# Stores of a routing table, issued by ScalarE in place of SP

## The chip, the cores and the metric

The program runs on one core of a Trainium2 chip. A core has TensorE (PE, matrix products), VectorE (DVE), ScalarE (ACT), GpSimd (POOL) and SyncE (SP). Each takes its instructions in order from a queue of its own, and they meet in semaphores. PE, DVE and ACT compute; SP only issues DMAs here, and ACT and POOL issue some too. The metric is device microseconds for one execution of the whole program, the median of several runs.

## The reference

The reference is a network on 512 tokens of width 1024, in float32: two blocks of modulated FFN, token mixing (gated MLP, differential attention, sparse attention) and FFN, then a second block whose feed-forward part is PEER, a choice among 16384 experts. The change lies in PEER, of which this is the core:

```python
q = (xf @ wq).reshape(t, PEER_HEADS, 2, PEER_DKEY // 2)
scores = jnp.einsum("thpc,hpnc->thpn", q, sub_keys)
s_top, i_top = lax.top_k(scores, PEER_TOPK)            # 16 of 128, two sides
cand_s = s_top[:, :, 0, :, None] + s_top[:, :, 1, None, :]
best_s, best_pos = lax.top_k(cand_s, PEER_TOPK)        # 16 experts a head
gates = jax.nn.softmax(best_s, axis=-1)
u = jnp.take(u_tab, expert_idx); vv = jnp.take(v_tab, expert_idx)
act = gelu(einsum("cd,chkd->chk", xc, u)) * gates
out = einsum("chk,chkd->cd", act, vv)
```

So each token has 8 heads with 16 experts each, 128 pairs of an expert number and a gate.

## The kernel before

A float32 product is done as three products of two halves: each weight tile of 512 KB is loaded by SP into `raw` (4 buffers), ACT copies its high half to `wh` (L265), DVE the rest to `wl` (L266), both with three buffers, and PE runs 24 matmuls for one projection (`proj`, L288): 8 with `yh` and `wh`, 8 with `yl` and `wh`, 8 with `yh` and `wl`.

The first 128 tokens fetch the rows of their experts (GpSimd's indirect loads `row`, DVE's products `vacc`). For the other 384 the kernel computes all 16384 experts, in 128 units of 128, and weights them with a gate that is zero for experts not chosen. In `peer()` the loop of L1855 to L1863 does this for the first 94 units while the gates are not yet known: a projection with the weights `pu`, the gelu `hg` on ACT, and a store `acts` of `hg` to DRAM, issued by ACT (L1859). Beside it, in portions, runs the generator `route()` that makes the gates.

`route()` lays the gates out as a table of 128 x 128 experts by token. It takes the 384 tokens in 6 blocks of 64. For 4 tokens of a block (a group, 16 in a block) DVE compares numbers and makes two selection matrices `o1` and `o2` (L1686, L1688; both stand as `o` in the rows), ACT scales the second by the gates, `og` (L1690, four instructions), PE multiplies both to `gp` in PSUM (L1697, four matmuls), and ACT copies `gp` into the block's tile `st` (L1698). `st` is 128 x 128 x 64 float32 with one buffer. At a block's end four stores of 1 MB each, `gates`, bring `st` to DRAM (L1711); that of the last block stays where it is. The next block's first copy into `st` has to wait until these stores have landed. Three groups are in flight at a time, as far as the buffers go. Later the gates are read back, by unit (`gs` L1847, `gq` L1892).

What runs when is set in two steps: by credits in Python, `routed()` and `gather()`, which say how many portions of `route()` and of the row fetch go with each projection, and by the scheduler of the language, which sets each engine's order from its own costs of the instructions. It places a store's issue as an instruction of the engine that issues it. There is no order written by hand.

Of the kernel before, what the change touches and what calls it, by code (L numbers as in the profile page):

```python
# [198 lines left out]
class Net:  # L199
# [1404 lines left out]
    def route(self, X, G, begun):  # L1604


        nc = self.nc
        best, pos, itop, numbers, iis = {}, {}, {}, {}, {0: self.ii0}
        for quad in range(4):
# [3 lines left out]
            for i in range(4):  # L1613
                q = self.x[4 + i]
# [4 lines left out]
            for t in range(NT):  # L1619
# [27 lines left out]
                if t == 0:  # L1647
                    yield from self.resolve(best[0], pos[0], itop[0], self.ii0, quad * 2, 2)
                    q = slice(quad * 32, quad * 32 + 32)
# [9 lines left out]
        for n, (t, a, b) in enumerate(BLOCKS):  # L1659
            for v in (t, BLOCKS[n + 1][0] if n + 1 < len(BLOCKS) else t):  # L1660
                if v not in iis:
                    iis[v] = self.blk(name="ii")
                    yield from self.resolve(best[v], pos[v], itop[v], iis[v], 0, 8)
            if t not in numbers:
                ii = iis[t]
                tp = self.bank("tp", "T")
                nc.tensor.transpose(tp[:, :P], ii[:, :P], self.ident)
                nc.tensor.transpose(tp[:, P:2 * P], ii[:, P:2 * P], self.ident)
                nc.tensor.transpose(tp[:, 2 * P:3 * P], best[t], self.ident)
                tr = self.blk(name="tr")  # L1670
                nc.vector.tensor_copy(tr[:, :384], tp[:, :384])
                trb = tr[:, 384:].bitcast(BF)[:, :P]
                nc.vector.tensor_copy(trb, tr[:, P:2 * P])
                numbers[t] = tr, trb
                yield "turn", 2
            tr, trb = numbers[t]
            st = self.stage.tile([P, NE, BT], F32, name="st", tag="st", bufs=1)
            left = []

            def four(v):  # L1680
                return v.rearrange("p (a b) -> p a b", b=P)

            for q in range(a, b, 4):
                o1, o2 = self.blk(name="o1"), self.tmp.tile([P, P, 4], BF, name="o2", tag="t", bufs=6)
                og = self.blk(name="og")
                nc.vector.tensor_tensor(four(o1), self.iota[:, None, :].to_broadcast([P, 4, P]),  # L1686
                                        tr[:, q:q + 4, None].to_broadcast([P, 4, P]), op=OP.is_equal)
                nc.vector.tensor_tensor(o2, self.iota4, trb[:, None, q:q + 4].to_broadcast([P, P, 4]), op=OP.is_equal)  # L1688
                for i in range(4):
                    nc.scalar.activation(og[:, i * P:(i + 1) * P], o2[:, :, i], AF.Copy,  # L1690
                                         scale=tr[:, 2 * P + q + i:2 * P + q + i + 1])

                def outer(o1=o1, og=og, q=q):
                    ps = self.bank("gp", "T")
                    for i in range(4):
                        c = slice(i * P, (i + 1) * P)
                        nc.tensor.matmul(ps[:, c], lhsT=o1[:, c], rhs=og[:, c], start=True, stop=True)  # L1697
                    nc.scalar.activation(st[:, :, q - a:q - a + 4], ps.rearrange("p (t e) -> p e t", t=4), AF.Copy)  # L1698

                left.append(outer)  # L1700
                if len(left) > 3:
                    left.pop(0)()
                yield "hot", 2
            for f in left:
                f()
                yield "late", 2
            if n == len(BLOCKS) - 1:
                self.last_gates = st
            else:
                for q in range(4):  # L1710
                    nc.sync.dma_start(G[:, n, q * 32:(q + 1) * 32], st[:, q * 32:(q + 1) * 32])  # L1711
                yield "late", 2

    def chosen(self, XN, acc):
# [288 lines left out]
```

## Time and profile before

| | us |
|---|---|
| median of 3 runs | 3659.66 (3652.52 to 3664.91) |
| the profiled execution | 3655.58 |
| its span, first to last instruction | 3653.8 |

The mean clock that TensorE was granted is 0.991 of full speed. The profile names engines and lines: "L1711" is line 1711 of the kernel, "st<-gp" an instruction that fills `st` from `gp`; a row of the timeline may stand for several like instructions ("x8"), and in brackets is the idle time ahead of it with what ended it. A matmul of the program in float32 can stand as two rows' instructions: a `gp` group of four is x8. "SPq" and "ACTq" are the issues of DMAs by SP and ACT. The stores in question are issued between 2686 and 2914 us; the loop with `route()` beside it runs until about 2940 us, and the last phase, with the gates read back, from there to the end.

### The profile page before, as it was taken

To read this page: it belongs to the slowest core of one execution; us is meant where nothing else is said; L and a number is where in the kernel's file an instruction comes from. 1 tells how busy PE (TensorE), PEld (TensorE's weight loads), DVE (VectorE), ACT (ScalarE), POOL (GpSimd) and SP (SyncE) were. 2 spreads that over 40 slices of the span, in tenths; PEclk is the share of its full clock that TensorE was granted. 3 is DMA by queue.
4 is the path that set the end of the run, shared out by engine and by line. 5 is a ranking of instruction groups with operands and counts; after the bars stand their busy time and mean duration, and the time that the engine had idled before them with its cause. 6 is when DMAs were issued, how large, how long until landed. Compare 5 with 4: busy or idle time off the path is not lost. (4 is left out here: it accounts for less than half of the span.)

```text
span 3653.8 us, 49253 instructions
## 1 busy us (share of the span) xinstructions
PE 3545.1 (97%) x18265; PEld 3011.7 (82%) x18265; DVE 2394.0 (66%) x4791; ACT 1564.9 (43%) x2770; POOL 371.1 (10%) x358
## 2 busy tenths in 40 slices
PE   7999999999999999999999999899999999999998
PEld 6888876788888888766888887788999999988886
DVE  6555587665563334776533377598998777788786
ACT  4332466433233323465433254333477753344333
POOL 0000100000000001000000000011331234432220
PEclk9999999999999999999999999999999999999999
DMA  7566330266653333400233321245887888899994
GB/s 250 185 187 200 113 100 18 64 197 195 199 187 104 98 91 111 128 30 24 93 93 95 100 84 64 75 147 187 270 292 287 302 280 315 311 338 355 328 325 143
DMA packets 260896, 636.49 MB, mean 174 GB/s; under 512 B 83696, under 2 KB 118816, under 8 KB 258096
## 3 DMA queue, kind: packets, MB, share of 16 engines
q1 hardware_dynamic: 207312, 474.35, 40.1%
q0 software_dynamic: 39808, 140.52, 11.2%
q10 hardware_dynamic: 13536, 18.49, 1.4%
q8 instruction: 143, 2.34, 0.3%
q14 instruction: 97, 0.79, 0.1%
HBM read 591.71 MB, written 41.55 MB: 173 GB/s over the span
## 5 line engine op out<-in xcount | busy, mean ns | idle before, releaser
L265 ACT ACTIVATE wh<-raw 128x1024 fp32r<-128x1024 f32 (+2 forms) x620 | 645.8, 1043 | 1135.2 <-PE proj L288 864.5
L266 DVE TENSOR_TENSOR wl<-raw,wh 128x1024 fp32r<-128x1024 f32 (+2 forms) x620 | 743.9, 1202 | 497.5 <-ACT wh L265 358.9
L288 PE MATMUL proj<-yh,wh 128*128 128x512 f32 (+1 forms) x2744 | 644.8, 374 | 6.0 <-ACT hg L1853 2.0
L288 PE MATMUL proj<-yh,wl 128*128 128x512 f32 (+1 forms) x2744 | 627.2, 370 | 11.7 <-DVE wl L266 11.6
L288 PE MATMUL proj<-yl,wh 128*128 128x512 f32 (+1 forms) x2744 | 628.9, 370 | 0.0
L288 PEld LDWEIGHTS proj<-yh,wl 128*128 128x128 f32 x2744 | 502.8, 188 | 83.0 <-DVE wl L266 15.4
L288 PEld LDWEIGHTS proj<-yh,wh 128*128 128x128 f32 x2744 | 499.5, 188 | 81.3 <-ACT hg L1853 3.3
L288 PEld LDWEIGHTS proj<-yl,wh 128*128 128x128 f32 x2744 | 503.8, 188 | 67.6
L540 DVE SCALAR_TENSOR_TENSOR scr<-raw,cact 128x1024 bf16<-128x1024 f32 x128 | 156.6, 1224 | 133.1 <-DMA raw<-in_wada 132.6
L1836 PE MATMUL acc<-wl,yh 128*128 128x512 f32 x756 | 234.2, 391 | 2.4 <-DVE wl L266 2.4
L1836 PE MATMUL acc<-wh,yh 128*128 128x512 f32 x756 | 233.8, 390 | 1.3 <-ACT wh L265 1.2
L1836 PE MATMUL acc<-wh,yl 128*128 128x512 f32 x756 | 233.3, 390 | 1.6 <-DVE yl L272 1.6
L1744 POOL DMA_INDIRECT row<-in_purows,c x128 | 156.5, 1223 | 521.5 <-DVE row L1728 276.8
L672 DVE TENSOR_TENSOR ga<-sg,proj 128x512 f32<-128x512 f32 x88 | 60.5, 687 | 227.0 <-PE proj L288 223.2
L1744 POOL DMA_INDIRECT row<-in_pv,c x128 | 167.0, 1305 | 371.0 <-DVE vacc L1736 245.3
L277 PE MATMUL proj<-yl,wh 128*128 128x256 f32 (+1 forms) x552 | 177.0, 330 | 10.8 <-DVE yl L399 7.1
L278 PE MATMUL proj<-yh,wl 128*128 128x256 f32 (+1 forms) x552 | 173.8, 323 | 2.2 <-DVE wl L266 2.2
L276 PE MATMUL proj<-yh,wh 128*128 128x256 f32 (+1 forms) x552 | 164.6, 328 | 7.8 <-ACT yh L645 6.3
L1836 PEld LDWEIGHTS acc<-wl,yh 128*128 128x128 f32 x756 | 141.2, 188 | 34.7 <-DVE wl L266 5.4
L1836 PEld LDWEIGHTS acc<-wh,yl 128*128 128x128 f32 x756 | 141.8, 188 | 32.1 <-DVE yl L272 2.1
L1836 PEld LDWEIGHTS acc<-wh,yh 128*128 128x128 f32 x756 | 141.2, 188 | 29.9 <-ACT wh L265 2.1
L1736 DVE SCALAR_TENSOR_TENSOR vacc<-row,act,vacc 128x1024 f32<-128x1024 f32 x127 | 162.6, 1280 | 0.7
(465 smaller groups left out, 5178.0 us busy)
## 6 DMA issues: line engine op xcount, KB each, us to landing
raw<-in_wada SPq DMA_DIRECT2D x144, 512.0 KB
raw<-in_pu SPq DMA_DIRECT2D x128, 512.0 KB
raw<-in_pv SPq DMA_DIRECT2D x128, 512.0 KB
raw<-in_wg SPq DMA_DIRECT2D x84, 512.0 KB
raw<-in_wu SPq DMA_DIRECT2D x84, 512.0 KB
raw<-in_wd SPq DMA_DIRECT2D x64, 512.0 KB
gates<-st SPq DMA_DIRECT2D x20, 1024.0 KB
acts<-hg ACTq DMA_DIRECT2D x94, 192.0 KB
```

Of the source, the lines that this page charges most:

```text
L265: nc.scalar.activation(h[:, :n], raw[:, :n], AF.Copy)
L266: self.latest = nc.vector.tensor_sub(l[:, :n], raw[:, :n], h[:, :n].bitcast(F32)).ins
L276: mm(out, lhsT=lh, rhs=rh, start=start, stop=False)
L277: mm(out, lhsT=lh, rhs=rl, start=False, stop=False)
L278: mm(out, lhsT=ll, rhs=rh, start=False, stop=stop)
L288: self.nc.tensor.matmul(ps, lhsT=w[:, k * P:(k + 1) * P], rhs=X[c + k][part], start=c + k + i == 0, stop=i == 2 and c + k == nk - 1)
L540: nc.vector.scalar_tensor_tensor(scr, raw, 1.0, self.cact, op0=OP.mult, op1=OP.mult, accum_out=self.mod[:, l, j:j + 1])
L672: nc.vector.tensor_mul(a, sg, p[1])
L1736: nc.vector.scalar_tensor_tensor(acc, row, a, acc, op0=OP.mult, op1=OP.add)
L1744: nc.gpsimd.indirect_dma_start(out=row, out_offset=None, in_=tables[kind], in_offset=bass.IndirectOffsetOnAxis(ap=self.experts[:GT, s:s + ...
L1836: nc.tensor.matmul(acc[q], lhsT=a[:, t * P:(t + 1) * P], rhs=half(w, m), start=q not in started, stop=end and i == 2)
```

## The change

The four stores of a block are issued by ACT instead of SP, 20 stores in all:

```diff
--- before.py
+++ after.py
@@ -1708,7 +1708,7 @@
                 self.last_gates = st
             else:
                 for q in range(4):
-                    nc.sync.dma_start(G[:, n, q * 32:(q + 1) * 32], st[:, q * 32:(q + 1) * 32])
+                    nc.scalar.dma_start(G[:, n, q * 32:(q + 1) * 32], st[:, q * 32:(q + 1) * 32])
                 yield "late", 2
 
     def chosen(self, XN, acc):
```

Besides the issue itself the scheduler now orders ACT, PE and DVE otherwise around each of the five stores. On SP the 20 issues are gone and nothing else moves, but that the first read of `gs` stands three loads earlier.

ACT around block 2's store, before. The names are: `og_23368` and on the groups of block 3, `st_23365` the tile of block 3, `hg_23387`, `hg_23448` and `hg_23515` the gelus of three projections, `wh_23586` and on the high halves of the weights of the next ones.

```order
L1690 ACTIVATE og_23377<-o2_23376,tr_23362 128x128 x4
L1853 ACTIVATE hg_23387<-proj_23388 128x384
L265 ACTIVATE wh_23586<-raw_23584 128x1024
L1859 DMA acts_19126<-hg_23387 128x384
L1690 ACTIVATE og_23423<-o2_23422,tr_23362 128x128 x4
L265 ACTIVATE wh_23638<-raw_23636 128x1024
L1853 ACTIVATE hg_23448<-proj_23449 128x384
L1859 DMA acts_19126<-hg_23448 128x384
L1690 ACTIVATE og_23432<-o2_23431,tr_23362 128x128 x4
L1690 ACTIVATE og_23484<-o2_23483,tr_23362 128x128 x4
L265 ACTIVATE wh_23705<-raw_23703 128x1024
L1698 ACTIVATE st_23365<-gp_23439 128x128x4
```

The splits `wh` of three units stand ahead of the first copy into the new tile `st_23365`.

The same place after the change, from the store on:

```order
L1711 DMA gates_19125<-st_22814 128x2048 x4
L1690 ACTIVATE og_23368<-o2_23367,tr_23362 128x128 x4
L1690 ACTIVATE og_23377<-o2_23376,tr_23362 128x128 x4
L1853 ACTIVATE hg_23387<-proj_23388 128x384
L1698 ACTIVATE st_23365<-gp_23439 128x128x4
L1859 DMA acts_19126<-hg_23387 128x384
L1690 ACTIVATE og_23423<-o2_23422,tr_23362 128x128 x4
L1690 ACTIVATE og_23432<-o2_23431,tr_23362 128x128 x4
L1853 ACTIVATE hg_23448<-proj_23449 128x384
L1698 ACTIVATE st_23365<-gp_23491 128x128x4
```

and, behind one more `acts` store:

```order
L1690 ACTIVATE og_23484<-o2_23483,tr_23362 128x128 x4
L1690 ACTIVATE og_23499<-o2_23498,tr_23362 128x128 x4
L1698 ACTIVATE st_23365<-gp_23506 128x128x4
L1853 ACTIVATE hg_23515<-proj_23516 128x384
L1698 ACTIVATE st_23365<-gp_23558 128x128x4
L1859 DMA acts_19126<-hg_23515 128x384
L1690 ACTIVATE og_23551<-o2_23550,tr_23362 128x128 x4
L1690 ACTIVATE og_23566<-o2_23565,tr_23362 128x128 x4
L1698 ACTIVATE st_23365<-gp_23573 128x128x4
L265 ACTIVATE wh_23586<-raw_23584 128x1024
```

The first copy into `st_23365` now stands one `hg` behind the store, and the split `wh_23586` stands behind five of these copies.

PE at the same place before, from the end of the projection that ran when block 2 was done; `o_23366` and on are groups of block 3:

```order
L288 MATMUL proj<-yh,wl 128x384 x8
L1697 MATMUL gp<-og,o_23366 128x128 x4
L288 MATMUL proj<-yh,wh 128x384 x8
L288 MATMUL proj<-yl,wh 128x384 x8
L288 MATMUL proj<-yh,wl 128x384 x8
L1697 MATMUL gp<-og,o_23375 128x128 x4
L1697 MATMUL gp<-og,o_23421 128x128 x4
L288 MATMUL proj<-yh,wh 128x384 x8
L288 MATMUL proj<-yl,wh 128x384 x8
L288 MATMUL proj<-yh,wl 128x384 x8
L1697 MATMUL gp<-og,o_23430 128x128 x4
L1697 MATMUL gp<-og,o_23482 128x128 x4
```

PE after, from the end of the second projection behind that place:

```order
L288 MATMUL proj<-yh,wh 128x384 x8
L288 MATMUL proj<-yl,wh 128x384 x8
L288 MATMUL proj<-yh,wl 128x384 x8
L1697 MATMUL gp<-og,o_23366 128x128 x4
L1697 MATMUL gp<-og,o_23375 128x128 x4
L1697 MATMUL gp<-og,o_23421 128x128 x4
L1697 MATMUL gp<-og,o_23430 128x128 x4
L1697 MATMUL gp<-og,o_23482 128x128 x4
L1697 MATMUL gp<-og,o_23497 128x128 x4
L1697 MATMUL gp<-og,o_23549 128x128 x4
L1697 MATMUL gp<-og,o_23564 128x128 x4
L288 MATMUL proj<-yh,wh 128x384 x8
```

The groups stood one or two between two projections of 24 matmuls; now three projections (two of them and the rest of one) stand in a row, eight groups follow together, and the next projection after them. Behind blocks 4 and 5 the order of ACT and PE is changed in the same way.

## Rows read from the trace of the kernel before

**Rows 1.** The page's busy time, share of the span, instructions.

```profile
PE 3545.1 (97%) x18265; PEld 3011.7 (82%) x18265; DVE 2394.0 (66%) x4791; ACT 1564.9 (43%) x2770; POOL 371.1 (10%) x358
```

**Rows 2.** Windows: busy us of PE, PEld, DVE, ACT, POOL; clock, DMA share, GB/s.

```profile
2660.00:2940.00 280.00, 270.13 (x1759) 267.99 (x1759) 228.47 (x369) 215.90 (x509) 66.49 (x53) 0.99 0.83 296
2960.00:3600.00 640.00, 634.67 (x2976) 545.96 (x2976) 504.80 (x665) 257.64 (x434) 198.28 (x161) 1.00 0.94 320
```

**Rows 3.** Waits of PE, 2660 to 2940: us in total, times, longest.

```profile
PE gp L1697 <- ACT st L1698: 4.9, 2, 3.2
PE gp L1697 <- ACT og L1690: 4.3, 1, 4.3
PE proj L288 <- ACT hg L1853: 0.6, 1, 0.6
```

**Rows 4.** Waits of SP's issues in the same stretch.

```profile
SPq L262 <- DVE wl L266: 213.0, 43, 14.5
SPq L1711 <- ACT st L1698: 8.7, 4, 3.1
```

**Rows 5.** Timeline of ACT at three stores: start, duration, instruction, idle before.

```profile
2760.94 1.06 ACT L265 ACTIVATE wh<-raw 128x1024 fp32r<-128x1024 f32 x1 [0.88 <-PE proj L288]
...
2764.22 1.08 ACT L1698 ACTIVATE st<-gp 128x512 f32<-128x512 f32 x2 [2.22 <-DMA gates<-st]
2765.19 1.31 ACT L1690 ACTIVATE og<-o,tr 128x128 f32<-128x128 bf16 x4
...
2766.88 0.49 ACT L1853 ACTIVATE hg<-proj 128x384 f32<-128x384 f32 x1
...
2875.63 1.09 ACT L1698 ACTIVATE st<-gp 128x512 f32<-128x512 f32 x2 [3.74 <-DMA gates<-st]
...
2927.02 1.08 ACT L1698 ACTIVATE st<-gp 128x512 f32<-128x512 f32 x2 [1.96 <-DMA gates<-st]
```

**Rows 6.** Timeline of SP's issues, 2640 to 2960.

```profile
2686.61 3.75 SPq L1711 DMA_DIRECT2D gates<-st  x4
...
2747.89 3.21 SPq L1711 DMA_DIRECT2D gates<-st  x4
2754.46 43.27 SPq L262 DMA_DIRECT2D raw<-in_pu  x8
...
2857.79 3.76 SPq L1711 DMA_DIRECT2D gates<-st  x4
...
2910.14 3.23 SPq L1711 DMA_DIRECT2D gates<-st  x4
```

**Rows 7.** Timeline of PE behind the stores of blocks 2, 4, 5.

```profile
2754.79 1.55 PE L288 MATMUL proj<-yh,wl 128*128 128x384 f32 x8
2756.18 1.95 PE L1697 MATMUL gp<-og,o 128*128 128x128 f32 x16
2757.88 1.63 PE L288 MATMUL proj<-yh,wh 128*128 128x384 f32 x8
...
2764.87 1.16 PE L1697 MATMUL gp<-og,o 128*128 128x128 f32 x8 [1.69 <-ACT st L1698]
2765.78 1.64 PE L288 MATMUL proj<-yh,wh 128*128 128x384 f32 x8
...
2877.19 1.65 PE L288 MATMUL proj<-yh,wh 128*128 128x384 f32 x8
...
2924.30 1.63 PE L288 MATMUL proj<-yh,wh 128*128 128x384 f32 x8
```

**Rows 8.** The page's groups: busy us, mean ns, idle before.

```profile
L266 DVE TENSOR_TENSOR wl<-raw,wh 128x1024 fp32r<-128x1024 f32 (+2 forms) x620 | 743.9, 1202 | 497.5 <-ACT wh L265 358.9
```

**Rows 9.** Windows of 2 us behind block 1's store, columns as in rows 2.

```profile
2694.00:2696.00 2.00, 2.00 (x14) 2.00 (x13) 2.00 (x4) 0.49 (x1) 0.00 (x0) 1.00 1.03 434
2700.00:2702.00 2.00, 2.00 (x13) 2.00 (x12) 2.00 (x3) 1.00 (x1) 0.00 (x0) 1.00 0.39 75
```

**Rows 10.** The DMA view from 2748 to 2764.

```profile
DMA packets 1298, 6.26 MB, mean 391 GB/s; under 512 B 130, under 2 KB 377, under 8 KB 785
```

## The prediction

> **What bounds the kernel now.** I read the busy shares first. TensorE (PE) is busy 97% of the span [rows 1]: the reader sees that a change counts only where PE waits for it. The windows come next [rows 2]. The stretch that holds the five stores has PE busy 270.13 of 280 us; the one behind it, up to the last tiles, 634.67 of 640. So the whole reserve of the first is 9.9 us, and no more than 5.3 us of a delay can be hidden later. Then the waits of PE in that stretch [rows 3]: 4.9, 4.3 and 0.6 us, all on ACT, none on a weight load or on VectorE's (DVE's) `wl`. Then those of SP [rows 4]: its weight loads wait 213.0 us in all for `wl`, that is for a free `raw` slot, in 43 waits; its stores wait 8.7 us for ACT's last `st`. So SP is ahead of need: the loads are limited by slots, not by the queue that the stores share with them.
>
> What ties ACT to the stores is `st` with one buffer. The first `st` copy of a block waits until the stores of the block before have landed (after 2.22, 3.74 and 1.96 us of waiting behind blocks 2, 4 and 5) [rows 5]. From a store's issue [rows 6] to that copy it is 2764.22 − 2747.89 = 16.3 us, 2875.63 − 2857.79 = 17.8 and 2927.02 − 2910.14 = 16.9. Before the change nothing suffers, because ACT does three splits `wh` and two `hg` that PE needs ahead of that copy, and PE works on projections meanwhile: behind blocks 2 and 4 it lost 1.69 and 3.2 us [rows 3, 7].
>
> **The change part by part.** *Removed:* 20 issues from SP, in five groups of four. PE waits for no load, so this is worth nothing by itself: a load starts when `wl` frees a slot, and behind block 2's store SP issued the next at 2754.46 [rows 6], with PE never short of one.
>
> *Added:* the same issues on ACT, each group of four 3.21 to 3.76 us on SP [rows 6], so 5 × 3.5 = 17.5 us. I price them at nothing on PE: they stand where ACT would wait for the landing a moment later anyway, with PE inside 70 projection matmuls (12.2 us at 1.39 us per 8, the pitch of [rows 7]). Without that cover they would cost 17.5 us.
>
> *Moved:* the order on ACT and PE, and this decides. The first `st` of the next block now stands one or two `hg` behind the store, with nothing between that PE needs: the splits `wh` that stood ahead of it (three, at block 3) are now behind it. While ACT waits for the landing, everything behind waits too: `hg`, `og`, then `wh`. PE has its projections in a row, then eight `gp` groups in a cluster, and then a unit whose `wh` stands on ACT behind all that feeds the cluster.
>
> Block 2 to 3. Behind the landing ACT has 5 `st` + 6 groups of 4 `og` + 2 `hg` + 1 `wh` until PE's next unit can start. Prices [rows 5]: `st` 0.53 (a pair less overlap 1.06), 4 `og` 1.31, `hg` 0.49, `wh` 1.06. Sum 2.65 + 7.86 + 0.98 + 1.06 = 12.55 us. With the landing at the old distance PE starts at 2764.22 + 12.55 = 2776.8. Before, it started this unit at 2765.78 [rows 7], with 5 of the 8 groups done (the first fence of PE in the section on the change); 3 more at 0.85 (1.70 for two, 2756.18 to 2757.88) make 2768.3. Difference +8.5.
>
> Block 4 to 5: the same rows in the same order. 2875.63 + 12.55 = 2888.2, against 2877.19 + 2.55 = 2879.7: +8.5.
>
> Block 5 to 6: in the order there, behind the landing come 4 `st`, 3 groups of `og`, one `hg`, one `wh`: 2.12 + 3.93 + 0.49 + 1.06 = 7.6; 2927.02 + 7.6 = 2934.6, against 2924.30 + 2.55 = 2926.9: +7.7.
>
> Block 1 to 2: four `hg` stand ahead of the first `st`, but PE no longer has `gp` groups to put between three units, and each unit's `wl` stands behind one other DVE operation of about a `wl`'s length, 1.2 us [rows 8]. Bounds: nothing, or 3 × 1.2 = 3.6 us. I take 3.6, since each of the three stands so.
>
> Block 3 to 4: before, PE waited 4.3 us there for `og` [rows 3]; after, the cluster is fed by the same chain of `og`. I take 0, between −4.3 (the wait goes) and +4.3 (once more).
>
> Sum: 8.5 + 8.5 + 7.7 + 3.6 = 28.3 us. The profiled execution took 3655.58 us, so 3683.9. It is 4.1 us under the median of the runs, 3659.66; by the median the same sum gives 3688. I say 3686.
>
> *The unknown in it* is when a store lands that has a queue beside the weight loads. Lower bound from rows: the highest rate of the stretch is 434 GB/s, but right behind block 1's store, issued at 2686.61, it falls to 75 GB/s at 2700 [rows 9], so that one was done in 13.4 us. With 13.4 in place of 16.3, 17.8 and 16.9 the sum loses 2.9 + 4.4 + 3.5 = 10.8: 3673 to 3677. Upper bound: from 2748 to 2764 6.26 MB moved at 391 GB/s [rows 10], 4.19 of them the store. If the three loads that stood behind it (1.57 MB) share the time, 7.83 MB take 20.0 us; +3.7 + 2.2 + 3.1 = +9.0: 3693 to 3697. I take the old distances, between the two and measured in the same place.
>
> **Rivals.** *(a) The store lands later.* It now shares the DMA engines with the loads packet by packet and no longer stands ahead of those issued behind it: 3695 by the upper bound. For it: the engines are 83% busy in the stretch [rows 2] and the loads find free slots. Against it: loads come only as PE uses slots up, and PE waits.
>
> The Trainium skill ("DMA: Bandwidth & Descriptors", section "Issuing engines are not separate DMA queues") states that starting transfers from several engines saves only the time of issue, because all run on the same 16 DMA engines and interleave; by its section "Queues, rings and completion order" each of these takes turns between the queues at packet granularity. By that rule the landing is not sooner than before and case (a) gets weight. No run here yet shows two such queues with large transfers against each other.
>
> *(b) No change.* The store, ahead of nothing, takes the whole rate: 4.19 MB at 434 GB/s [rows 9] is 9.7 us. The sum loses 6.6 + 8.1 + 7.2 = 21.9 and leaves +6: 3664 at the median, inside 0.3%. For it: that rate is on record. Against it: no store was that quick.
>
> *(c) The other side: SP was what held PE up.* If the loads behind the stores come late and ACT's splits with them, all of PE's waits of the stretch go: 3655.58 − 9.9 = 3645.7, or 3650 by the median. It decides only where the landing and 12.55 us of ACT behind it end by 2768.3, so with a landing at 2755.7, 7.9 us after the issue, which needs 4.19 MB / 7.9 us = 530 GB/s. Against it: SP's loads wait for slots 213 us, and the highest rate of the rows is 434.
>
> **How the numbers follow.** My forecast 0.62; (a) 0.20; (b) 0.13; (c) 0.05. About 0.3%, 11 us, is what a measurement of this kernel can tell from no change. The forecast with its bounds and (a) lie above that, (b) within; (c) counts as faster although its price is just at the limit. Faster 0.05, same 0.13, slower 0.82. The range goes from 3664, where (b) ends, to 3702, (a) with block 3's +4.3 and some 3 us of the spread of the runs (3652.52 to 3664.91).
>
> **What would show it.** Right: PE's waits for `og`, `st` and `wh` in the stretch come to 30 us or more, from 9.8, in three clumps behind the stores of blocks 2, 4 and 5; the first `st` behind each of these stores waits about 9 us for the landing; the window to 2940 loses about 10% of its PE share, the one behind it nothing. Wrong: the first `st` comes less than 10 us behind the issue (b, c); or PE waits for `hg` or `wh` at once behind the issue, so that the 17.5 us of issue on ACT are not covered; or PE waits for `wl` and DVE for `raw`, so that the loads come late.

## The result, and the profile after

The changed kernel takes 3683.16 us (median of 5 runs, 3679.93 to 3688.45), the kernel before 3658.75 in the same runs; the ratio is 1.0067, 95% interval 1.0055 to 1.0079. That is 24.4 us slower. 3686 was forecast. The profiled execution took 3680.88 us, its span is 3678.8 (before: 3653.8).

The windows show where the 25 us are. One pair takes the same piece of work in both kernels, from 2.1 us behind the end of ACT's last copy into `st` of block 1 (2686.58 before, 2688.70 after) to the start of the gelu of the 94th projection; the third line answers to the second of [rows 2]. First the kernel before (columns as in [rows 2]):

```profile
2688.69:2964.60 275.91, 266.04 (x1733) 264.01 (x1732) 221.49 (x351) 210.30 (x497) 65.39 (x53) 0.99 0.83 294
```

and the changed kernel:

```profile
2690.81:2988.65 297.84, 274.74 (x1733) 270.08 (x1732) 221.07 (x351) 209.41 (x496) 79.29 (x53) 0.98 0.75 272
2985.00:3625.00 640.00, 635.44 (x2970) 544.53 (x2969) 504.05 (x663) 257.07 (x432) 197.01 (x161) 1.00 0.95 319
```

The same 1733 matmul rows take 21.9 us more: PE's idle time goes from 9.9 to 23.1 us, and its busy time from 266.0 to 274.7. The last phase is as busy as before (635.44 of 640) and gives nothing back. The other 3 us of the two profiled executions stand mostly ahead of the first store (2.1 us by ACT's last copy of block 1) and are not of the change: of the runs below, this place lay between 2.4 us earlier and 5.9 us later in those whose program is the same up to there.

PE's waits in the changed kernel, 2660 to 2980, against [rows 3]:

```profile
PE gp L1697 <- ACT og L1690: 17.8, 10, 5.7
PE proj L288 <- ACT wh L265: 3.9, 4, 1.0
PE proj L288 <- DVE wl L266: 1.4, 2, 1.0
```

All but 1.4 us is still for ACT, now for `og`, and for the first time for `wh`. The place behind block 2's store, ACT's timeline:

```profile
2751.64 3.81 ACTq L1711 DMA_DIRECT2D gates<-st  x4
2755.50 2.49 ACT L1690 ACTIVATE og<-o,tr 128x128 f32<-128x128 bf16 x8 [3.88 <-DVE o L1688]
2757.90 0.47 ACT L1853 ACTIVATE hg<-proj 128x384 f32<-128x384 f32 x1
2766.42 0.60 ACT L1698 ACTIVATE st<-gp 128x512 f32<-128x512 f32 x1 [8.05 <-DMA gates<-st]
...
2776.93 1.04 ACT L265 ACTIVATE wh<-raw 128x1024 fp32r<-128x1024 f32 x1
```

and PE's:

```profile
2763.19 1.95 PE L1697 MATMUL gp<-og,o 128*128 128x128 f32 x16
2767.36 5.92 PE L1697 MATMUL gp<-og,o 128*128 128x128 f32 x32 [2.22 <-ACT og L1690]
2774.51 2.58 PE L1697 MATMUL gp<-og,o 128*128 128x128 f32 x16 [1.23 <-ACT og L1690]
2778.03 1.68 PE L288 MATMUL proj<-yh,wh 128*128 128x384 f32 x8 [0.94 <-ACT wh L265]
```

ACT stands 8.05 us for the landing, 14.8 us behind the issue (16.3 before), and has the split `wh` that PE's next unit needs done 11.5 us after that. PE's last six groups go at the pace of ACT's `og`, and it waits for `wh`. Behind block 4 the same rows come again, 15.5 us from issue to landing (ACT, then PE):

```profile
2871.57 4.47 ACTq L1711 DMA_DIRECT2D gates<-st  x4
...
2887.11 0.60 ACT L1698 ACTIVATE st<-gp 128x512 f32<-128x512 f32 x1 [8.15 <-DMA gates<-st]
...
2897.60 1.04 ACT L265 ACTIVATE wh<-raw 128x1024 fp32r<-128x1024 f32 x1
```

```profile
2898.70 1.49 PE L288 MATMUL proj<-yh,wh 128*128 128x384 f32 x7 [0.94 <-ACT wh L265]
```

Behind block 5 it is not so plain. ACT stands for its own issue and for PE first, and only 0.60 us for the landing, which comes 14.9 us behind the issue at 2928.98; the splits are again behind the copies:

```profile
2933.08 1.00 ACT L1690 ACTIVATE og<-o,tr 128x128 f32<-128x128 bf16 x3 [3.84 <-issue]
...
2940.77 0.41 ACT L1690 ACTIVATE og<-o,tr 128x128 f32<-128x128 bf16 x1 [3.35 <-PE gp L1697]
...
2943.89 0.60 ACT L1698 ACTIVATE st<-gp 128x512 f32<-128x512 f32 x1 [0.60 <-DMA gates<-st]
```

The table below carries the rest. For each run it compares the end of ACT's last copy into `st` of each block, and the start of the 94th gelu, with the kernel before (all read from ACT's timeline of the profiled execution); a column is what is lost from one such point to the next, so what happens behind that store. A negative number is a gain.

| run | behind store 1 | 2 | 3 | 4 | 5 | sum |
|---|---|---|---|---|---|---|
| changed kernel | 1.6 | 5.5 | 4.5 | 5.1 | 5.2 | 21.9 |
| e1, GpSimd issues | −0.1 | 6.1 | −0.2 | 1.6 | 1.2 | 8.6 |
| e2, SP, late `wh` | 0.2 | 3.0 | 1.9 | 3.2 | 4.6 | 12.9 |
| e3, ACT, small | −0.1 | −2.0 | −1.1 | −3.5 | 0.0 | −6.7 |
| e4, SP, small | 0.0 | −2.0 | −1.3 | −3.5 | 0.0 | −6.8 |
| e5, ACT a quarter | 0.0 | 2.5 | −1.2 | 1.3 | 0.1 | 2.6 |
| e6, ACT half | 0.0 | 9.2 | 0.1 | 7.9 | 5.3 | 22.4 |
| e7, ACT, small, late `wh` | 0.2 | 0.2 | 3.5 | −1.0 | 2.4 | 5.3 |
| e8, not block 3 | 1.6 | 5.5 | 1.4 | 5.1 | 4.8 | 18.3 |
| e9, SP, two halves | 1.8 | −2.0 | −0.1 | −3.5 | 0.0 | −3.7 |
| e10, ACT, two halves | 10.0 | 5.2 | 7.8 | 1.9 | 4.1 | 29.0 |
| e11, ACT, written ahead | 4.0 | 2.1 | 2.1 | 3.2 | 6.4 | 17.8 |
| e12, SP, written ahead | −1.9 | 9.2 | −2.1 | 1.0 | 0.8 | 6.9 |

### The profile page after: what moved, and what is told of

Same layout as the page of the kernel before. It is cut to its first block, busy times and chain, and to the rows that moved or that the text cites. A ratio compares the mean times of both kernels' runs of the same rounds, so it can differ in the third digit from the quotient of the medians.

```text
span 3678.8 us, 49251 instructions
## 1 busy us (share of the span) xinstructions
PE 3557.9 (97%) x18265; PEld 3019.2 (82%) x18265; DVE 2393.9 (65%) x4791; ACT 1564.2 (43%) x2770; POOL 385.3 (10%) x358
## 5 line engine op out<-in xcount | busy, mean ns | idle before, releaser
L1744 POOL DMA_INDIRECT row<-in_purows,c x128 | 170.3, 1331 | 522.2 <-DVE row L1728 296.2
```

Source lines behind the costliest of these rows:

```text
L1744: nc.gpsimd.indirect_dma_start(out=row, out_offset=None, in_=tables[kind], in_offset=bass.IndirectOffsetOnAxis(ap=self.experts[:GT, s:s + ...
```

## The experiments

Theory O: the time is lost by the order that ACT and PE have once ACT issues the stores; a copy that waits for a landing stands ahead of the splits that PE needs next. Rival E: the issue itself, on ACT, costs it. Rival Q: a queue other than SP's is the worse one.

### e1, GpSimd issues the stores

```diff
-                    nc.sync.dma_start(G[:, n, ...
+                    nc.gpsimd.dma_start(G[:, n, ...
```

> The stores are issued by GpSimd: off SP's queue as in the changed kernel, but ACT's order is nearly that of the kernel before (three splits wh ahead of the first st copy behind the stores of blocks 2 and 4). Theory O (the changed order on ACT and PE costs the time): 3651 to 3667 us, PE's waits in the stretch of the stores 8 to 18 us. Rival Q (a queue of its own beside the weight loads is what costs, or SP's queue was the better one): about 3683 us as in the changed kernel, with the loads or the landing late.

Measured: 3662.4 us, ratio 1.0005 (0.9996 to 1.0014). Off SP's queue, with ACT's order nearly that of before, the loss is 0.14%, 5 us, at most by the interval: Q falls as the main cause of the 24 us. The profiled execution, at 3666.98 us one of the slowest of the eleven, has 8.6 us in the table. PE's waits in the stretch:

```profile
PE gp L1697 <- ACT st L1698: 9.3, 3, 5.2
PE gp L1697 <- ACT og L1690: 4.2, 1, 4.2
PE proj L288 <- ACT hg L1853: 0.6, 1, 0.6
```

They are 14.1 us, from 9.8: the landing is later. GpSimd issued block 2's store and ACT came to the next copy so:

```profile
2750.44 2.18 POOL L1711 DMA_DIRECT2D gates<-st  x4
```

```profile
2770.77 1.08 ACT L1698 ACTIVATE st<-gp 128x512 f32<-128x512 f32 x2 [5.74 <-DMA gates<-st]
```

20.3 us, close to the 20.0 that rival (a) of the prediction gave for a store that shares the engines with the loads. The DMA view of 2750 to 2771 has the sharing, 5.83 MB on the store's queue (4.19 the store) and 1.81 MB on SP's:

```profile
DMA packets 1958, 8.27 MB, mean 394 GB/s; under 512 B 206, under 2 KB 605, under 8 KB 1445
q0 software_dynamic: 1024, 5.83, 71.1%
q1 hardware_dynamic: 490, 1.81, 21.2%
```

### e2, SP issues, but the splits are late

`self.copied` is the fifth copy into a block's `st` (`c` in the code, from the second block on); every split written later is ordered behind it on ACT.

```diff
...
-        nc.scalar.activation(h[:, :n], raw[:, :n], AF.Copy)
+        with self.tc.issue_after(self.copied) if self.copied is not None else ExitStack():
+            nc.scalar.activation(h[:, :n], raw[:, :n], AF.Copy)
...
+                    if n and q - a == 16:
+                        self.copied = c.ins
```

> The stores stay on SP, but the splits wh of units traced behind the fifth copy of a block are ordered behind that copy on ACT, as the changed kernel has them behind blocks 2 and 4. Theory O: 12 to 20 us slower than before, 3671 to 3679 us: behind the landing ACT does 5 st, 3 groups of og, one hg and one wh (7.8 us) before PE's next unit, so +3.7 each behind blocks 2 and 4, about +6 behind block 5 and up to +5 behind 1 and 3. Rival E (the issue on ACT, or its queue, costs the time): 3659 us within 5, since SP issues.

Measured: 3668.76 us, ratio 1.0025 (1.0015 to 1.0035). With SP issuing, the late splits alone cost 0.25%, 9 to 10 us; E, which expected nothing, falls as the only cause. The size is under the 12 to 20 us expected, by the medians; in the stretch itself the trace has 12.9. PE waits for `wh` here too:

```profile
PE gp L1697 <- ACT og L1690: 9.6, 6, 5.4
PE gp L1697 <- ACT st L1698: 4.2, 2, 2.5
PE proj L288 <- ACT wh L265: 2.8, 3, 0.9
```

It is less than in the changed kernel: behind the landing of block 2's store ACT has three groups of `og` to do ahead of the split, not six.

### e3 and e4, small stores, by ACT and by SP

Both keep 20 issues, of 64 KB each; the gates of the other experts are left out.

```diff
+                    nc.scalar.dma_start(G[:, n, q * 2:q * 2 + 2], st[:, q * 32:q * 32 + 2])   # e4: nc.sync
...
+        G = self.dram.tile([P, last, 8, BT], F32, name="gates")
...
```

> ACT issues 20 stores as in the changed kernel, but each of 2 of the 32 rows (64 KB); the gates of the other experts are left out and the later reads take the stored ones. ACT's order is then near that of before. Theory O: 3648 to 3660 us, as the issue on ACT is covered and no landing is waited for. Rival E (issue of 3.2 to 3.8 us a block on ACT stands on PE's path): 5 x 3.5 us more, 3670 us or above.

> The same small stores, issued by SP: the partner of the run with small stores on ACT. Theory O: 3648 to 3656 us (PE's two waits for st, 4.9 us, go, the 4.3 us for og stay), within 4 us of the run on ACT. Rival E: about 17 us faster than the run on ACT.

Measured: 3652.41 us on ACT, ratio 0.998 (0.9971 to 0.9989), and 3650.93 on SP, 0.9979 (0.997 to 0.9988). No difference that can be measured. ACT's order is only in part that of before: behind blocks 2 and 4 of e3 the first copy stands ahead of all splits, as in the changed kernel, but two splits follow behind it and one group of `og`; in e4 one split stands ahead. With that order and next to no landing, 20 issues on ACT cost PE nothing, though each group of four still takes ACT some 2 us, as behind block 2 in the run on ACT:

```profile
2748.22 2.05 ACTq L1711 DMA_DIRECT2D gates<-st  x4
```

And both are about 7 us under the kernel before: that is what the waits for the landing, and the order around them, cost it (the table has the gain behind stores 2 to 4). The issues here are shorter than the 3.8 us of the full stores, so that E is bounded rather than excluded by this pair.

### e5 and e6, ACT issues one or two of the four

```diff
-                    nc.sync.dma_start(G[:, n, ...
+                    (nc.scalar if q == 3 else nc.sync).dma_start(G[:, n, ...    # e6: q > 1
```

> ACT issues only the last of a block's four stores, SP the other three. ACT's order keeps two splits wh between the store and the next block's first copy. Theory O (order): 3654 to 3663 us. Rival E (the share that ACT issues counts, 24.4 us for all): a quarter, +6 us, 3665 us.

> ACT issues two of a block's four stores, SP two. ACT's order is then that of the changed kernel behind blocks 2, 4 and 5 (no split wh ahead of the first copy), and that of before behind block 3. Theory O: the changed kernel's time less the 4.5 us of block 3, 3674 to 3682 us. Rival E: half, +12 us, 3671 us, or less.

Measured: 3658.78 us, ratio 0.9993 (0.9984 to 1.0002), and 3679.39 us, 1.0055 (1.004 to 1.007). A quarter costs nothing, a half four fifths of the whole. That is no share of an issue cost; it is the order, which keeps two splits ahead of the copy in e5 and none in e6 (behind blocks 2 and 4). The table says it more sharply: behind those blocks ACT of e6 spends 0.85 us on its two issues, where the changed kernel spends 3.81 and 4.47 on four, and yet e6 loses more there, 9.2 and 7.9 us against 5.5 and 5.1. PE's order there is not quite that of the changed kernel; the runs do not show why e6 loses more. PE's waits for `og` in the stretch, e5:

```profile
PE gp L1697 <- ACT og L1690: 9.5, 3, 4.2
```

and e6:

```profile
PE gp L1697 <- ACT og L1690: 22.1, 7, 6.0
PE proj L288 <- ACT wh L265: 2.8, 3, 0.9
```

### e7, small stores by ACT, with late splits

The edits of e2 and e3 together.

> ACT issues 20 small stores (64 KB, the gates of the other experts left out), and the splits of the units traced behind a block's fifth copy are ordered behind that copy, near the order of the changed kernel behind blocks 2, 4 and 5. There is next to no landing to wait for. Theory O with the landing as the carrier: 3651 to 3660 us, since ACT starts on the copies 10 us earlier. If the order by itself (PE's eight groups in a cluster fed by ACT) carried the time: 3668 us or more.

Measured: 3663.65 us, ratio 1.0011 (1.0002 to 1.0019), above the range that was expected for the landing as the only carrier. Against e3, which has the same stores and early splits, it is 11.2 us more (10.2 when each is set against the kernel before in its own runs): the late order costs that much with next to no landing to wait for. Against the changed kernel it is 19.5 us less. Behind blocks 2 and 4, where ACT has the changed kernel's five copies and six groups of `og` ahead of the split, the table parts the loss: over e3 the late order costs 2.2 and 2.5 us, and the changed kernel, with the landing in front, 5.3 and 6.1 more. PE's order in e7 has some groups between the projections again, so that these last figures hold the landing and that difference together. So the order has two prices: groups of PE that go at ACT's pace, and, most likely the larger one, the landing that stands in front of them.

### e8, the changed kernel without block 3

```diff
+                    (nc.sync if n == 2 else nc.scalar).dma_start(G[:, n, ...
```

> As the changed kernel, but the stores of block 3 stay on SP, and ACT's order behind block 3 is then near that of before. If block 3's loss of 4.5 us in the changed kernel is of its changed order: 3677 to 3681 us. If it is something carried over from the other blocks: 3683 us as in the changed kernel.

Measured: 3675.76 us, ratio 1.0044 (1.0032 to 1.0056), a little under the range. By the table the loss behind store 3 goes from 4.5 to 1.4 us and the others stay: it belongs to block 3's own stores, and is not carried over. By the medians the gain is 7.4 us; the table holds 3.6 of it. e8 takes issue and order away together there, but the changed kernel's trace tells them apart: ACT waits for DVE's selection matrices, long after the issue (2808.22, 4.11 us) is over,

```profile
2822.70 0.41 ACT L1690 ACTIVATE og<-o,tr 128x128 f32<-128x128 bf16 x1 [6.97 <-DVE o L1688]
```

and what the order does is seen in PE's timeline:

```profile
2823.16 4.15 PE L1697 MATMUL gp<-og,o 128*128 128x128 f32 x16 [5.72 <-ACT og L1690]
2826.95 2.43 PE L288 MATMUL proj<-yh,wl 128*128 128x384 f32 x8
...
2837.01 1.66 PE L288 MATMUL proj<-yh,wh 128*128 128x384 f32 x8 [1.04 <-ACT wh L265]
```

### e9 and e10, two half tiles in two buffers

A block's tile is two tiles of 32 tokens, two buffers in the same 32 KB a partition, each stored when its 8 groups are done. The gates lie in DRAM by halves and are read in pieces of 128 bytes.

```diff
+                if (q - a) % 32 == 0:
+                    sts.append(self.stage.tile([P, NE, BT // 2], F32, name="st", tag="st", bufs=2))
...
+                            nc.sync.dma_start(G[:, n, m, v:v + 32], st[:, v:v + 32])    # e10: nc.scalar
```

> SP issues the stores, but a block's tile is two tiles of 32 tokens in two buffers (the same 32 KB), each stored when its 8 groups are done, so no copy waits for a landing for long; later the gates are read back in pieces of 128 bytes where it was 256. Theory O: the blocks lose no wait for st, about 7 us less than before in the stretch of the stores, as with the small stores; in all 3650 to 3656 us if the last phase hides the smaller pieces, more if not (its DMA engines are 94% busy), which the windows tell apart.

> The same with ACT issuing the 40 stores. ACT's order behind several of them has the late splits again, but with two buffers there is no landing to wait for. Theory O (landing in front of late splits is the cost): 2 to 12 us over the run with SP, the price of the order alone. Rival E (the issue on ACT): 40 x 4 stores of less size, some 20 to 30 us over the run with SP.

Measured: 3689.4 us, ratio 1.0079 (1.0063 to 1.0096), and 3725.03 us, 1.0179 (1.0162 to 1.0196). In e9 the stretch of the stores gains 3.7 us, less than the 7 expected, and the last phase does not hide the smaller pieces, nor the ten reads of `gs` that stand for one (160 of 32 KB, 16 of 320 KB before); the run does not part the two. Its window of e9, against 634.67 of 640 in [rows 2]:

```profile
2960.00:3640.00 680.00, 655.39 (x2988) 551.28 (x2987) 507.73 (x663) 263.28 (x547) 192.75 (x160) 0.99 0.96 302
```

e10 is 35.6 us over e9. Theory O had 2 to 12, rival E 20 to 30: here O's number is wrong and E's is near. (There are 40 stores, in ten groups of four.) One place shows how an issue can cost: ACT's timeline of e10 has the last of a group of issues ahead of three splits,

```profile
2690.24 1.15 ACTq L1702 DMA_DIRECT2D gates<-st  x1
2691.43 2.95 ACT L265 ACTIVATE wh<-raw 128x1024 fp32r<-128x1024 f32 x3 [1.22 <-issue]
```

and PE waits for the first of them:

```profile
2692.54 2.93 PE L288 MATMUL proj<-yh,wh 128*128 128x384 f32 x8 [5.75 <-ACT wh L265]
```

Of these 5.75 us the last issue is 1.22; the rest ACT spends on copies, a table load of 1.28 us with the other three issues beside it, an activation and the split itself. In the whole stretch of 2660 to 2990 the trace puts 7.5 us of ACT's idle time down to issues:

```profile
ACT og L1691 <- issue: 3.7, 1, 3.7
ACT wh L265 <- issue: 3.1, 2, 1.9
ACT L1858 <- issue: 0.7, 1, 0.7
```

So the issues by themselves do not make up the 35.6 us, and E's number is near without its cause being shown. The order differs from e9's in many places at once (PE waits 14.2 us for `og` and 10.4 for `wh` between 2660 and 2990, 6.0 and nothing in e9), and the 35.6 us are not split further here. What stands is that an issue on ACT is not free everywhere.

### e11 and e12, the weights written two units ahead

```diff
+            while ahead and len(ready) <= 2 and j + len(ready) < NE:
+                ready.append(self.unit(A["pu"][j + len(ready)].rearrange("p k m -> p (k m)")))
+            ps = self.proj(A["pu"][j], dense, n=n, pre=ready.pop(0) if ready else None)
```

> The changed kernel (ACT issues all stores), with each projection's weights written two units earlier in the program, so that behind blocks 2 and 4 ACT has PE's next split wh behind one st copy and two groups of og (0.5 + 2.4 + 1.1 = 4 us behind the landing) where it was behind 11.6 us. Theory O: 5 to 7 us less behind each of these blocks, some 2 behind block 5: 3666 to 3673 us. Rival E or Q (the issue on ACT, or its queue, costs): 3680 us or more, as nothing of that is changed.

> The same earlier writing of the weights in the kernel before (SP issues). Its order behind the stores stays with two or three splits ahead of the first copy. Theory O: 3655 to 3662 us, the control for the run with ACT; were it several us faster, the gain of that run would not be its order behind the stores.

Measured: 3704.81 us, ratio 1.0125 (1.0108 to 1.0142), and 3690.74 us, 1.0093 (1.0076 to 1.011). Both are far off, for a reason that has nothing to do with the stores: ahead of the first of them, from 2350 to 2680, both have the row

```profile
PE proj L288 <- DVE wl L266: 28.2, 4, 11.3
```

where the kernel before waits 11.6 us; by ACT's last copy of block 1 they are 30.4 and 25.6 us behind it. The totals thus tell nothing. Behind stores 2 to 4, where the split came forward, e11 loses 2.1, 2.1 and 3.2 us against the changed kernel's 5.5, 4.5 and 5.1: the direction of O, but behind blocks 2 and 4 it is 3.4 and 1.9 us less where 5 to 7 were expected, and behind stores 1 and 5 it is more. e12 adds a case: SP issued block 2's store and ACT's copy came 24.6 us later,

```profile
2772.09 3.27 SPq L1711 DMA_DIRECT2D gates<-st  x4
```

```profile
2796.67 1.09 ACT L1698 ACTIVATE st<-gp 128x512 f32<-128x512 f32 x2 [8.43 <-DMA gates<-st]
```

and 9.2 us were lost with the early order: splits ahead of the copy cover a landing only as long as they last. None of the versions that compute the whole beats the kernel before; e1 and e5 are level with it.

## Why the prediction was right, and where its sizes were not

**The mechanism.** Right behind blocks 2 and 4: the first copy of the next block waits for the landing 8.05 and 8.15 us (about 9 were forecast), all that PE needs from ACT waits behind it, and PE loses the time in clumps. Behind block 5 the splits are late too, but the landing holds ACT for 0.60 us only. e5 and e6, e1 and e2 show that the loss comes with the order.

**Removed from SP: worth nothing.** Right. SP's timeline has one row of loads through the stretch where [rows 6] had the stores in between,

```profile
2639.76 285.26 SPq L262 DMA_DIRECT2D raw<-in_pu  x47
```

and PE gains nothing by it; it waits 1.4 us for `wl`, which it did not before.

**Added to ACT: priced at nothing.** Right for this kernel, though the five groups took 20.2 us on ACT and not 17.5. Behind blocks 2 and 4 ACT waits some 8 us for the landing afterwards, behind block 5 for PE (3.35 us) and the landing (0.60), behind block 3 for DVE; e6 loses as much with issues a fifth as long, e3 against e4 bounds it for short ones, and e10 shows a place where it would have been wrong.

**Blocks 2, 4 and 5: 8.5, 8.5 and 7.7 forecast, 5.5, 5.1 and 5.2 measured.** The step that was mis-sized is the landing. It was put at the old 16.3, 17.8 and 16.9 us behind the issue; it came after 14.8, 15.5 and 14.9. That is 1.5, 2.3 and 2.0 us of the 3.0, 3.4 and 2.5 that are missing. Most of the rest is ACT's work behind it, 11.5 us in place of 12.55 behind blocks 2 and 4 (eight `og` in 2.48, not 2.62) and 7.0 in place of 7.6 behind block 5. The DMA view of 2751 to 2767 of the changed kernel shows what it had beside it:

```profile
DMA packets 967, 5.49 MB, mean 343 GB/s; under 512 B 118, under 2 KB 151, under 8 KB 455
q10 hardware_dynamic: 615, 4.25, 63.8%
q1 hardware_dynamic: 128, 0.46, 8.0%
```

6.26 MB moved before in the same 16 us [rows 10], 5.49 now. Only 1.3 MB go beside the store, 0.46 of them weights, where it was 2.1. SP issues no load from 2749.02 to 2779.26: a load needs a slot of `raw`, a slot comes free with DVE's `wl`, `wl` needs ACT's `wh`, and ACT, held up, makes none from 2747.39 to 2776.93. Rival (a)'s sharing is real, as e1's 20.3 us show, but in the changed kernel it is limited by the very wait it would have lengthened. The Trainium skill's rule ("DMA: Bandwidth & Descriptors", section "Issuing engines are not separate DMA queues"), that several issuing engines share the same DMA engines and save issue time alone, agrees with both: the store of the changed kernel landed sooner with fewer bytes beside it, and e1's later with more.

**Block 1: 3.6 forecast, 1.6 measured.** The upper bound was taken, three waits for `wl` of 1.2 us; two came, 1.4 us in all.

**Block 3: 0 forecast, between −4.3 and +4.3; 4.5 measured.** This term was wrong, and just outside its bounds. The wait for `og` was there before, and comes from DVE; in the changed order a unit's last eight products were left behind it, with the cluster of groups ahead of the next split, so that PE waits 5.72, 1.12 and 1.04 us where it had 4.25.

**The sum** was 28.3 us and is 21.9 in the trace, 24.4 by the medians. The errors of blocks 2, 4 and 5 (−8.9) and block 1 (−2.0) are partly made up by block 3 (+4.5). That the forecast of 3686 came within 3 us of 3683.16 is thus in part luck. (In rival (b) 3659.66 and 6 make 3666 by the median, not 3664; it changes no more than the lower end of the range.)

**What was to be seen.** PE's waits for `og`, `st` and `wh` were forecast at 30 us or more, in three clumps; they are 21.7, and 23.1 with `wl`. By place they are 4.4 us behind store 2, 7.8 behind 3, 5.9 behind 4 and 3.1 behind 5, so that the largest clump is one that was not forecast. PE's share from 2660 to 2940 was to fall by about 10%; its busy time falls from 270.13 to 260.08 us, 3.6 points. The other 8.7 us of the loss are inside PE's busy time, where the rows overlap less: the groups of a cluster go at ACT's pace, 1.29 us each (2.58 for two, above) and not 0.85, though a single `gp` row hardly changes (292 ns in the mean, 282 before), and the clock fell behind some of the waits.

What the runs don't tell: why the scheduler puts the splits behind the copies once ACT issues two of the four stores, and not for one. The order was read, and its cost measured; its cause in the scheduler's rules was not tried.

## What to carry to other kernels

Before moving a DMA's issue to another engine, compare the order of that engine and of those it feeds: the cost here was not the issue but a buffer's wait for its landing that came to stand ahead of work the busiest engine needed. A wait for a landing on an in-order engine is cheap only while independent work for the bound engine stands in front of it; count what is queued behind, and set the work in front against how long the landing takes: e12 lost 9.2 us behind one store with the early order, when its landing took 24.6. And a queue whose loads wait for buffers to come free is not relieved by taking other transfers off it.

## What the runs showed of the hardware

PE's granted clock, 0.98 in the mean of the stretch, was 0.50, the lower of its two levels (1.2 of 2.4 GHz), right behind a wait of 5.72 us, and 1.00 again in the window from 2833, in the changed kernel:

```profile
2810.00:2823.00 13.00, 7.43 (x43) 7.11 (x42) 13.00 (x23) 0.80 (x2) 0.00 (x0) 0.96 0.69 292
2823.00:2827.00 4.00, 3.84 (x17) 3.55 (x17) 4.00 (x8) 3.24 (x12) 0.52 (x1) 0.50 0.57 179
2833.00:2837.00 4.00, 2.57 (x16) 2.37 (x16) 0.36 (x3) 4.00 (x12) 0.00 (x0) 1.00 0.15 53
```

Two groups that take 1.95 us in [rows 7] took 4.15 there. The kernel before has the same at this place: 0.50 from 2814.2 to 2820, behind its wait of 4.25 us. And a store of 4.19 MB took longer the more bytes moved beside it, at 389 to 394 GB/s: 16.3 us with 6.26 MB in all, 20.3 with 8.27 (e1), 24.6 with 9.72 (e12, the DMA view of 2772 to 2797). In the changed kernel it was 14.8 with 5.49 (343 GB/s in the mean, with the engines idle at the end). The view of e12:

```profile
DMA packets 2435, 9.72 MB, mean 389 GB/s; under 512 B 276, under 2 KB 758, under 8 KB 1921
```
